# A hybrid decoder layer on one core: the corner of a triangular inverse started later between the products, its turned operand loaded first

## The chip, the cores and the metric

The kernel runs on one NeuronCore of a Trainium2 chip. The core has a matrix engine (TensorE, PE in the profile, with PEld for its weight loads), a vector engine (VectorE, DVE), a scalar engine (ScalarE, ACT), GpSimd (POOL) and a sync engine (SyncE, SP) that mostly issues DMA transfers. Each engine runs its own instructions in order, and semaphores order them between engines. The metric is the device time of one execution in microseconds (us). The kernel before took 2265.33 us, the median of three runs (2264.02, 2265.33 and 2266.41).

## The reference

The layer has 1024 tokens of width 1024. It is a SwiGLU half-step, then a mixer of three branches (an RWKV-7 recurrence, sliding-window attention, attention into 256 memory tokens) that are merged by sigmoid gates, then another SwiGLU half-step, with normalisation around each.

```python
g_a, g_b, g_c = _split(jax.nn.sigmoid(gate_logits + gate_b[l]), (D, D, D))
merged = (g_a * (y_a @ w_branch[l, 0]) + g_b * (y_b @ w_branch[l, 1])
          + g_c * (y_c @ w_branch[l, 2]))
```

The recurrence that gives `y_a` is, for each token,

```python
sa = jnp.einsum('bhvk,bhk->bhv', state, a_t)
state = (state * w_t[:, :, None, :] + sa[..., None] * b_t[:, :, None, :]
         + v_t[..., None] * k_t[:, :, None, :])
```

The kernel computes it in 16 chunks of 64 tokens. Within a chunk the terms in `sa` make a triangular system of 64 equations for each of 8 heads, so 128 inverses of 64 by 64 triangular matrices are needed before the chunks can be walked in turn.

## The kernel before, in words

All of this lies in `mixer`. After the projections that feed the recurrence come seven **pairs** of column strips (`win_pair`, numbers 0 to 6; the pairs from 3 on are gates, 24 and up in `WIN_PAIRS`). A pair is computed by a Strassen-like scheme: seven **products** ("b11", "b21", "t2", "t1", "t3", "b22", "t4"), each of 12 matmuls of 128 by 512 (four blocks of the contraction, three matmuls each in `mm3`, lines 376 to 378, which emulate full float32 by high and low parts). They accumulate in the PSUM tiles `px`, `py` and `pz`. When a product is done, `kept` (line 1425, ACT) copies a partial sum to a `part` tile, or `made` (line 1432, DVE, then 1435, ACT) adds it to a kept one and writes half of an output tile `att`. The output tiles are two per pair from a pool of two, so an `att` tile of one pair cannot be written before the store of the same tile of the pair before has landed (line 1454, SP). The weights of each product come through `operands`: a load of `w_raw` (line 290, SP, five buffers), for the Strassen sums three or four DVE additions (lines 326, 327, 328 and 332), a cast to `w_hi` (line 299, ACT) and a subtraction to `w_lo` (line 301, DVE), eight operands ahead of their use. A `w_raw` load is issued when the buffer is free, which is when the last `w_lo` made from it is done.

The inverses are built beside these products. `rwkv_invert` solves, on DVE, the two diagonal 32 by 32 blocks of all 128 matrices during pairs 0 to 3, stores them in `inv_d`, and stores one of them transposed in `turn_d`. `rwkv_corner` then makes the remaining corner block as a product of three 32 by 32 blocks on PE. It loads `up` (from `ab_d`), `low` (from `inv_d`) and `turned` (from `turn_d`), four transfers each on SP (line 1176), every one in runs of 32 numbers, 128 bytes. The matmuls are cut into eight **lumps**: four of `iturned` with `iup`, whose result ACT copies to `ihalf`, and four of `ilow` with `ihalf`, whose result `icorner` goes back into `inv_d` in four transfers on the ACT queue (line 1190). `win_pair` calls `between()` after each product, which gives one lump, and `issue_after` keeps the next product of the pair behind that lump. `CORNER = (4, 5)` puts the lumps into pair 4: one after each of its seven products, the eighth right behind the seventh.

Then the pool `chunks` is opened, pair 5 runs, `chunk_fetch` asks for the first two chunks' tiles (`f`, 640 KB, line 1195; `dinv`, the inverse, two transfers of 64 KB, line 1197), and pair 6 runs. `rwkv_chain` walks the 16 chunks: each step is a row of small matmuls (line 1210) and a transposition (line 1249) with short DVE, ACT and POOL work between, and while that runs, matmuls of two plain gate strips (`pgate`) fill PE.

What stands in which order on an engine is decided by a scheduler in the language's tile layer: program order by default, `high_priority` moves things ahead, `issue_after` and `keep_in_program_order` bind them, and a product that is ready may be pulled ahead of one that is not. The order of the built program is fixed; at run time each engine works down its list.

Of the kernel before, what the change touches and what calls it, by code (L numbers as in the profile page):

```python
# [1 line left out]

# [1 line left out]

# [41 lines left out]
BRANCHES = (0, 2, 1)  # L46
ATT_BLOCKS = (18, 19, 14, 15, 16, 17, 20, 21, 22, 23)
GATES_PLAIN = 2
CORNER = (4, 5)
GATES_FIRST = 10  # L50
GATES_EARLY = 12
LUMPS = (29, 52)
# [2 lines left out]
WIN_PAIRS = ((16, 17), (20, 21), (22, 23)) + tuple((24 + g, 25 + g) for g in range(GATES_PLAIN, GATES_FIRST, 2))  # L55
# [6 lines left out]
H = C // 2  # L62
# [168 lines left out]
class Builder:  # L231
# [934 lines left out]
    def rwkv_corner(self, pool, ab_d, inv_d, turn_d):  # L1166

        nc = self.nc
        flat = lambda d: d.rearrange("c p q s t -> (c p q) s t")
        groups = [slice(g * H, (g + 1) * H) for g in range(P // H)]  # L1170
        up, turned, low, half, corner = (pool.tile([P, H, H], F32, name="i" + n, bufs=1) for n in ("up", "turned", "low", "half", "corner"))
        urgent = lambda: self.tc.high_priority(offset=self.urgent)
        with urgent():
            for t, d in ((up, flat(ab_d)[:, :H, H:]), (low, flat(inv_d)[:, H:, H:]), (turned, turn_d)):
                for g in groups:
                    nc.sync.dma_start(t[g], d[g].rearrange("i s t -> s i t"))
        for w, x, out in ((up, turned, half), (half, low, corner)):
            for a in range(0, H, H // 4):
                if a % (H // 2) == 0:
                    ps = self.psum("corner").rearrange("p (i t) -> p i t", t=H)  # L1180
                with urgent():
                    for i in range(a, a + H // 4):
                        for g in groups:
                            mm = self.tc.keep_in_program_order(nc.tensor.matmul(ps[g, i % (H // 2)], w[g, i], x[g, i], start=True, stop=True))
                    if a % (H // 2):
                        nc.scalar.copy(out[:, a - H // 4 : a + H // 4], ps)
                yield mm
        with urgent():
            for g in groups:
                nc.scalar.dma_start(flat(inv_d)[g, :H, H:].rearrange("i s t -> s i t"), corner[g])  # L1190
# [549 lines left out]
    def mixer(self, u, cp, close_raws, att_d, gate_d, km_d, vm_d):  # L1740
        nc, tc, io = self.nc, self.tc, self.io
        pk_d = tc.dram_tile([NC_, P, NPAIR, 5 * C], F32, name="pk_d")
        ab_d = tc.dram_tile([NC_, NPAIR, 2, C, C], F32, name="ab_d")
        inv_d = tc.dram_tile([NC_, NPAIR, 2, C, C], F32, name="inv_d")
        turn_d = tc.dram_tile([P, H, H], F32, name="turn_d")
# [17 lines left out]
        with tc.tile_pool(reuse_waits="tile", name="gates", bufs=2) as gp:  # L1763
            out = lambda: gp.tile([P, T], F32, tag="gate", name="att", bufs=2)
            with sums, tc.tile_pool(reuse_waits="tile", name="mix_xa", bufs=4) as pools["xa"]:
                fs = self.mix_forms(u, forms, loads)
            with tc.tile_pool(reuse_waits="tile", name="inv", bufs=1) as pool:
# [9 lines left out]
                for _ in inverse:  # L1777
                    pass
            for i in range(1, CORNER[0]):
                self.win_pair(i, fs, out, att_d, gate_d)  # L1780
            with tc.tile_pool(reuse_waits="tile", name="corner", bufs=1) as pool:
                corner = self.rwkv_corner(pool, ab_d, inv_d, turn_d)
                for i in range(*CORNER):
                    self.win_pair(i, fs, out, att_d, gate_d, lambda: next(corner))
                for _ in corner:
                    pass
            chunks = contextlib.ExitStack()
            early = chunks.enter_context(tc.tile_pool(reuse_waits="tile", name="chunks", bufs=2))
            self.win_pair(CORNER[1], fs, out, att_d, gate_d)
            fetched = [self.chunk_fetch(early, c, pk_d, inv_d) for c in (0, 1)]  # L1790
            for i in range(CORNER[1] + 1, len(WIN_PAIRS)):
                self.win_pair(i, fs, out, att_d, gate_d)
            over.close()
            with chunks, tc.tile_pool(reuse_waits="tile", name="chain", bufs=2) as pool:
                y = pool.tile([P, NPAIR, T], F32, name="y", bufs=1)
# [274 lines left out]
```

## Time and profile before

| | |
|---|---|
| median of three runs | 2265.33 us (2264.02 to 2266.41) |
| the profiled execution | 2265.33 us, of which the span is 2263.3 us |
| busy in the span | PE 98%, PEld 81%, DVE 73%, ACT 46%, POOL 3% |
| chain that ended last | PE 91%, DVE 4%, DMA 2%, ACT 1% |
| DMA | 431.90 MB, 191 GB/s over the span |
| mean granted clock of TensorE | 0.996 |

The page of a profile gives busy times, the span cut into slices, the chain of work that ended last and the costliest groups of instructions. The other views are of the same execution: the waits (who waited for whom, in all, how often, the longest), the timeline (start, duration, engine, line, operation, output and inputs, and in brackets the idle time before and what ended it), and the windows (busy time of each engine in a stretch, with the granted clock as a share of full speed and the busy share of the DMA engines). A matmul's row shows its duration with its latency, so the pace of a product is read from the distance of its starts.

### The profile page before, as it was taken

Reading aid. Unit: us, or ns where it says so; the run is one execution under the profiler, and the core shown is the slowest. Engines: PE = TensorE matmul, PEld = TensorE weight load, DVE = VectorE, ACT = ScalarE, POOL = GpSimd, SP = SyncE. Lnnn points to the kernel's source line nnn. Section 1 sums busy time; section 2 is a strip of 40 time slices with the busy share of each in tenths; the row PEclk is TensorE's granted clock in tenths of the full one; section 3 lists DMA queues with packets and bytes.
Section 4 is the critical chain, followed back from the end, with each engine's and each line's share of the span. In section 5 each row is a group of like instructions: output and inputs, shape, how many; then the busy total and the mean of one; then the engine's idle time right before and its main releaser. Section 6 shows DMA issues by size and latency. Waiting matters only on the chain.

```text
span 2263.3 us, 34508 instructions
## 1 busy us (share of the span) xinstructions
PE 2228.9 (98%) x12304; PEld 1832.7 (81%) x12304; DVE 1642.9 (73%) x2761; ACT 1031.4 (46%) x1933; POOL 59.3 (3%) x114
## 2 busy tenths in 40 slices
PE   8999999999999999979999999999999999999998
PEld 6888888888887788868888887788888888888887
DVE  6988767766698888853667567784898886656576
ACT  6523333454556654334445454434663223345451
POOL 0000000000000000000331000000000000000000
PEclk9999999999999999989999999999999999999999
DMA  8565666686665356455437877564565552357663
GB/s 292 172 202 167 202 212 215 228 291 205 193 208 195 111 159 195 149 154 166 147 107 248 271 255 263 178 211 135 171 214 176 196 189 103 115 167 250 203 195 122
DMA packets 279132, 431.90 MB, mean 191 GB/s; under 512 B 58512, under 2 KB 96912, under 8 KB 278704
## 3 DMA queue, kind: packets, MB, share of 16 engines
q1 hardware_dynamic: 266160, 409.96, 56.0%
q10 hardware_dynamic: 12800, 19.73, 2.7%
q8 instruction: 97, 1.59, 0.3%
q14 instruction: 75, 0.61, 0.1%
HBM read 292.75 MB, written 135.79 MB: 189 GB/s over the span
## 4 chain that ended last, share of the span: by engine, by line
PE 91%; DVE 4%; DMA 2%; ACT 1%; issue 1%; SPq 1%; DVEq 0%; ACTq 0%
PE px L376 9%; PE px L378 9%; PE px L377 9%; PE po L376 6%; PE po L377 6%; PE po L378 6%; PE pz L376 4%; PE pz L377 4%; PE pz L378 4%; PE pgate L376 2%; PE pgate L378 2%; PE pgate L377 2%; PE pr L376 2%; PE pr L377 2%; PE pr L378 2%; PE pb L376 2%
## 5 line engine op out<-in xcount | busy, mean ns | idle before, releaser
L299 ACT CAST w_hi<-w_raw 128x512 fp32r<-128x512 f32 x608 | 377.0, 622 | 734.9 <-PE px L377 178.8
L301 DVE TENSOR_TENSOR w_lo<-w_raw,w_hi 128x512 fp32r<-128x512 f32 x608 | 418.6, 690 | 184.1 <-ACT w_hi L299 165.1
L376 PE MATMUL po<-u,w_hi 128*128 128x512 f32 (+1 forms) x476 | 180.9, 380 | 0.0
L378 PE MATMUL po<-u,w_lo 128*128 128x512 f32 (+1 forms) x476 | 180.9, 380 | 0.0
L377 PE MATMUL po<-u,w_hi 128*128 128x512 f32 (+1 forms) x476 | 180.9, 380 | 0.0
L376 PE MATMUL px<-u,w_hi 128*128 128x512 f32 x380 | 148.0, 390 | 0.8 <-DVE km L1595 0.8
L376 PE MATMUL pz<-u,w_hi 128*128 128x512 f32 x380 | 148.0, 389 | 0.0
L378 PE MATMUL px<-u,w_lo 128*128 128x512 f32 x380 | 147.9, 389 | 0.0
L377 PE MATMUL px<-u,w_hi 128*128 128x512 f32 x380 | 147.8, 389 | 0.0
L378 PE MATMUL pz<-u,w_lo 128*128 128x512 f32 x380 | 147.8, 389 | 0.0
L377 PE MATMUL pz<-u,w_hi 128*128 128x512 f32 x380 | 147.8, 389 | 0.0
L376 PE MATMUL px<-f,w_hi 128*128 128x512 f32 x352 | 137.1, 390 | 0.0
L378 PE MATMUL px<-f,w_lo 128*128 128x512 f32 x352 | 137.0, 389 | 0.0
L377 PE MATMUL px<-f,w_hi 128*128 128x512 f32 x352 | 136.9, 389 | 0.0
L485 DVE TENSOR_TENSOR u<-hid,u 128x512 fp32r<-128x512 f32 x114 | 78.5, 691 | 43.4 <-ACT u L484 42.2
L378 PEld LDWEIGHTS po<-u,w_lo 128*128 128x128 f32 x476 | 89.5, 188 | 17.1
L377 PEld LDWEIGHTS po<-u,w_hi 128*128 128x128 f32 x476 | 89.5, 188 | 17.0
L376 PEld LDWEIGHTS po<-u,w_hi 128*128 128x128 f32 x476 | 89.5, 188 | 16.8
L376 PE MATMUL pgate<-u,w_hi 128*128 128x512 f32 x256 | 103.0, 402 | 0.0
L378 PE MATMUL pgate<-u,w_lo 128*128 128x512 f32 x256 | 101.7, 397 | 0.0
L484 ACT CAST u<-hid 128x512 fp32r<-128x512 f32 x114 | 70.9, 622 | 65.1 <-DMA hid<-form_d 58.4
L377 PE MATMUL pgate<-u,w_hi 128*128 128x512 f32 x256 | 99.9, 390 | 0.0
(453 smaller groups left out, 5169.3 us busy)
## 6 DMA issues: line engine op xcount, KB each, us to landing
w_raw<-in_ffn_in SPq DMA_DIRECT2D x224, 256.0 KB
hid<-form_d SPq DMA_DIRECT2D x154, 256.0 KB
w_raw<-in_win SPq DMA_DIRECT2D x112, 256.0 KB
form_d<-g SPq DMA_DIRECT2D x88, 256.0 KB
w_raw<-ffn_sum_d SPq DMA_DIRECT2D x88, 256.0 KB
form_d<-h SPq DMA_DIRECT2D x66, 256.0 KB
w_raw<-in_ffn_out SPq DMA_DIRECT2D x66, 256.0 KB
first_d<-first SPq DMA_DIRECT2D x48, 256.0 KB
```

The lines of the kernel that those rows point to most:

```text
L299: self.nc.scalar.copy(hi, x)
L301: self.split_last = self.nc.vector.tensor_tensor(lo, x, hi.bitcast(F32), ALU.subtract)
L376: mm(out, wh, xh, start=first, stop=False, **kw)
L377: mm(out, wh, xl, start=False, stop=False, **kw)
L378: self.last_mm = mm(out, wl, xh, start=False, stop=last, **kw)
L484: self.nc.scalar.copy(hi, x)
L485: self.nc.vector.tensor_tensor(lo, x, hi.bitcast(F32), ALU.subtract)
```

## The change

`CORNER` becomes `(4, 4)`: its first number is still the pair at which the corner begins, its second is now a number of products. The lumps become a chain of four empty entries and then the corner's steps. Pairs 4 and 5 both draw from it after each product, so that the corner starts in the middle of pair 4 and runs on into pair 5. The pool of the corner's tiles stays open until pair 5 has been written down, the pool `chunks` is opened after it, and the first two chunks are fetched in the program just ahead of pair 6, the last. Inside `rwkv_corner` the loads are written `up`, `turned`, `low` where they were `up`, `low`, `turned`. The arithmetic is the same.

```diff
+import itertools
-CORNER = (4, 5)
+CORNER = (4, 4)
...
-            for t, d in ((up, flat(ab_d)[:, :H, H:]), (low, flat(inv_d)[:, H:, H:]), (turned, turn_d)):
+            for t, d in ((up, flat(ab_d)[:, :H, H:]), (turned, turn_d), (low, flat(inv_d)[:, H:, H:])):
                 for g in groups:
                     nc.sync.dma_start(t[g], d[g].rearrange("i s t -> s i t"))
...
             with tc.tile_pool(reuse_waits="tile", name="corner", bufs=1) as pool:
-                corner = self.rwkv_corner(pool, ab_d, inv_d, turn_d)
-                for i in range(*CORNER):
-                    self.win_pair(i, fs, out, att_d, gate_d, lambda: next(corner))
-                for _ in corner:
-                    pass
+                lumps = itertools.chain(itertools.repeat(None, CORNER[1]), self.rwkv_corner(pool, ab_d, inv_d, turn_d))
+                for i in range(CORNER[0], len(WIN_PAIRS) - 1):
+                    self.win_pair(i, fs, out, att_d, gate_d, lambda: next(lumps, None))
+                assert next(lumps, None) is None
             chunks = contextlib.ExitStack()
             early = chunks.enter_context(tc.tile_pool(reuse_waits="tile", name="chunks", bufs=2))
-            self.win_pair(CORNER[1], fs, out, att_d, gate_d)
             fetched = [self.chunk_fetch(early, c, pk_d, inv_d) for c in (0, 1)]
-            for i in range(CORNER[1] + 1, len(WIN_PAIRS)):
-                self.win_pair(i, fs, out, att_d, gate_d)
+            self.win_pair(len(WIN_PAIRS) - 1, fs, out, att_d, gate_d)
```

The scheduler makes more of this than the diff tells. Line numbers in the changed program are one higher up to the end of `rwkv_finish` and its neighbours (L376 is now L377).

**The corner's start, on PE.** Rows of matmuls with buffer numbers; only the first of each product's 12 is shown. `px_9254`, `py_9255`, `pz_9256` are pair 4's sums. Before:

```order
L376 MATMUL px_9254<-u_5952,w_hi_9119 128x512
...
L1184 MATMUL corner_9300<-iturned_9284,iup_9283 32x32 x32
L376 MATMUL py_9255<-u_5976,w_hi_9137 128x512
...
L1184 MATMUL corner_9300<-iturned_9284,iup_9283 32x32 x32
L376 MATMUL px_9254<-mix_form_8232,w_hi_9159 128x512
```

Now, with `px_9515` the first product of pair 5:

```order
L377 MATMUL px_9254<-mix_form_8248,w_hi_9195 128x512
...
L377 MATMUL px_9515<-u_5952,w_hi_9267 128x512
...
L1185 MATMUL corner_9376<-iturned_9360,iup_9359 32x32 x32
L377 MATMUL pz_9256<-u_6661,w_hi_9214 128x512
...
L1185 MATMUL corner_9376<-iturned_9360,iup_9359 32x32 x32
L377 MATMUL px_9254<-mix_form_8256,w_hi_9232 128x512
```

The first lump stood behind the first product of pair 4. It now stands behind five products of pair 4 and the first of pair 5, which was pulled ahead. Behind the first lump come "b22" of pair 4, the second lump, and "t4" of pair 4.

**The same place on SP**, where the rows are the issued transfers. Before, from the corner's loads to the first chunk tile:

```order
L1176 DMA iup<-ab_d 32x32x32 x4
L1176 DMA ilow<-inv_d 32x32x32 x4
L1176 DMA iturned<-turn_d 32x32x32 x4
L1454 DMA gate_d<-att 128x1024
L290 DMA w_raw<-in_win 128x512 x4
L1454 DMA gate_d<-att 128x1024 x2
L1195 DMA f<-pk_d 128x1280
```

Now:

```order
L1177 DMA iup<-ab_d 32x32x32 x4
L1177 DMA iturned<-turn_d 32x32x32 x4
L1177 DMA ilow<-inv_d 32x32x32 x4
L291 DMA w_raw<-in_win 128x512 x4
L1455 DMA gate_d<-att 128x1024 x3
L291 DMA w_raw<-in_win 128x512 x3
L1455 DMA gate_d<-att 128x1024
L291 DMA w_raw<-in_win 128x512 x5
L1455 DMA gate_d<-att 128x1024
L291 DMA w_raw<-in_win 128x512
L1196 DMA f<-pk_d 128x1280
```

The store of pair 3's second output tile stood right behind the corner's loads; four weight loads are ahead of it now. The first chunk tile stood behind four weight loads, and stands behind thirteen.

**The outputs of pair 4, on DVE.** `att<-py`, `att<-px` and `att<-pz` are line 1432 (now 1433) after the products "b21", "t3" and "b22". Before:

```order
L1432 TENSOR_TENSOR att<-py,part 128x512
L301 TENSOR_TENSOR w_lo<-w_raw,w_hi 128x512
L301 TENSOR_TENSOR w_lo<-part,w_hi 128x512
L301 TENSOR_TENSOR w_lo<-w_raw,w_hi 128x512
L1432 TENSOR_TENSOR att<-px,part 128x512
L301 TENSOR_TENSOR w_lo<-w_raw,w_hi 128x512
L1432 TENSOR_TENSOR att<-pz,part 128x512
```

Now:

```order
L302 TENSOR_TENSOR w_lo<-part,w_hi 128x512
L302 TENSOR_TENSOR w_lo<-w_raw,w_hi 128x512 x3
L1433 TENSOR_TENSOR att<-pz,part 128x512
L302 TENSOR_TENSOR w_lo<-w_raw,w_hi 128x512
L327 TENSOR_TENSOR part<-w_raw 128x512
L328 TENSOR_TENSOR w_raw<-w_raw 128x512
L329 TENSOR_TENSOR w_raw<-part,w_raw 128x512
L1433 TENSOR_TENSOR att<-px,part 128x512
```

`att<-px`, which reads what "t3" has summed and has to be done before "t4" may add to `px`, stood ahead of `att<-pz`; it stands behind it and behind four more instructions.

**The chain's last step on PE.** Before:

```order
L1249 MATMUL bkt<-ident,f 128x128 x4
L378 MATMUL pgate<-u,w_lo 128x512
L376 MATMUL pgate<-u,w_hi 128x512
L377 MATMUL pgate<-u,w_hi 128x512
L378 MATMUL pgate<-u,w_lo 128x512
L376 MATMUL pgate<-u,w_hi 128x512
L377 MATMUL pgate<-u,w_hi 128x512
L1210 MATMUL z<-sv,gz 64x64 x8
L1210 MATMUL y<-gz,uv 64x64 x8
```

Now:

```order
L1211 MATMUL z<-uv,bk 64x64 x8
L1250 MATMUL bkt<-ident,f 128x128 x4
L1211 MATMUL z<-sv,gz 64x64 x8
L1211 MATMUL y<-gz,uv 64x64 x8
L1211 MATMUL y<-f,sv 64x64 x8
```

Eleven `pgate` matmuls are pulled ahead into pair 6 (three behind its third product in the built order, eight behind its fourth). They are missing at the chain's end: the last step has none of its six, the step before has two, and one is missing behind the last step.

## The prediction

> **What bounds the kernel now.** I read the page first, then the waits of PE, then the windows and the timeline around the largest wait, and last the queues that the change reorders.
>
> ```profile
> PE 2228.9 (98%) x12304; PEld 1832.7 (81%) x12304; DVE 1642.9 (73%) x2761; ACT 1031.4 (46%) x1933; POOL 59.3 (3%) x114
> PE 91%; DVE 4%; DMA 2%; ACT 1%; issue 1%; SPq 1%; DVEq 0%; ACTq 0%
> PE corner L1184 <- DMA iturned<-turn_d: 11.7, 4, 10.2
> PE var L1336 <- DVE ysq_lo L1326: 0.8, 1, 0.8
> 1000.00:1010.00 10.00, 2.34 (x65) 1.88 (x66) 0.00 (x0) 0.00 (x0) 0.00 (x0) 0.53 1.08 153
> 1010.00:1020.00 10.00, 10.00 (x157) 7.62 (x157) 1.98 (x3) 2.93 (x5) 0.00 (x0) 0.79 0.09 28
> 1020.00:1030.00 10.00, 10.00 (x226) 7.73 (x225) 2.69 (x5) 3.56 (x6) 0.00 (x0) 1.00 0.16 54
> ```
>
> PE is busy for 98% of the span and carries 91% of the chain that ended last, so a stall of PE is paid in full. The largest is in the corner: 11.7 us, waiting for the gather of `turned`; the next one near it is 0.8 us. In the windows (PE, PEld, DVE, ACT and POOL busy, granted clock, DMA share) all engines stand still in 1000 to 1010 while DMA is full at 1.08, and the clock is 0.53 there and 0.79 in the next window: the stall also costs pace after it. The timeline gives both parts.
>
> ```profile
> 993.10 0.39 PE L376 MATMUL px<-u,w_hi 128*128 128x512 f32 x1
> 995.59 0.39 PE L378 MATMUL px<-u,w_lo 128*128 128x512 f32 x1
> 1006.19 0.31 PE L1184 MATMUL corner<-iturned,iup 32*32 32x32 f32 x2 [10.21 <-DMA iturned<-turn_d]
> 1008.58 1.05 PE L1184 MATMUL corner<-iturned,iup 32*32 32x32 f32 x58 [0.31 <-DMA iturned<-turn_d]
> 1009.57 0.80 PE L376 MATMUL py<-u,w_hi 128*128 128x512 f32 x1
> 1014.64 0.75 PE L1184 MATMUL corner<-iturned,iup 32*32 32x32 f32 x64
> 1018.28 0.75 PE L1184 MATMUL corner<-iturned,iup 32*32 32x32 f32 x64
> 1021.91 0.75 PE L1184 MATMUL corner<-iturned,iup 32*32 32x32 f32 x64
> ```
>
> A product is 12 matmuls; its first and last start 2.49 us apart, so one takes 2.49 / 11 = 0.2265 us and the product 2.72. From lump 3 to lump 4 a lump and a product take 1021.91 - 1018.28 = 3.63, so a lump costs 0.91. The first product of pair 4 is through at 993.10 + 2.72 = 995.82. From there to lump 3 stand two lumps and two products, 7.26 us of work; they took 1018.28 - 995.82 = 22.46. **The stall costs 15.2 us**, 2.35 of them because the product between lumps 1 and 2 took 1014.64 - 1009.57 = 5.07 instead of 2.72.
>
> **The change, part by part.** *The later start.* The first lump now stands behind six products (five of pair 4 and the first of pair 5, which the scheduler pulls ahead): 993.10 + 6 x 2.72 = 1009.42. Even as the last of the twelve gathers, `turned` had landed by 1008.6 (the last bracket above).
>
> ```profile
> 992.79 5.19 SPq L1176 DMA_DIRECT2D iup<-ab_d  x4
> 998.02 3.41 SPq L1176 DMA_DIRECT2D ilow<-inv_d  x4
> 1001.47 3.76 SPq L1176 DMA_DIRECT2D iturned<-turn_d  x4
> 1005.34 0.86 SPq L1454 DMA_DIRECT2D gate_d<-att  x1
> 1016.12 14.82 SPq L290 DMA_DIRECT2D w_raw<-in_win  x4
> ```
>
> *The order of loads* puts `turned` 3.45 us earlier (1001.47 - 998.02), so by about 1005.2, with 4 us to spare. `low` takes its place, by 1008.6, and is needed with lump 5, some 10 us later. The full 15.2 us go, in the clock too: eight lumps of work stay, and the two that now stand back to back were back to back before.
>
> *What takes its place, at "t4" of pair 4.* DVE must have read `px` (`att<-px`) before "t4" may add to it, and in the new order that row stands behind `att<-pz`, a `w_lo` and three weight sums. All of these wait for "b22". The pace of DVE is in these rows:
>
> ```profile
> 993.73 0.69 DVE L301 TENSOR_TENSOR w_lo<-w_raw,w_hi 128x512 fp32r<-128x512 f32 x1 [1.86 <-ACT w_hi L299]
> 994.33 0.69 DVE L326 TENSOR_TENSOR part<-w_raw 128x512 f32<-128x512 f32 x1
> 997.05 0.69 DVE L327 TENSOR_TENSOR w_raw<-w_raw 128x512 f32<-128x512 f32 x1
> 997.77 0.69 DVE L328 TENSOR_TENSOR w_raw<-part,w_raw 128x512 f32<-128x512 f32 x1
> 1025.55 0.75 PE L1184 MATMUL corner<-ilow,ihalf 32*32 32x32 f32 x64
> 1025.71 0.69 DVE L1432 TENSOR_TENSOR att<-px,part 128x512 f32<-128x512 f32 x1 [2.57 <-PE px L378]
> 1026.32 0.68 DVE L301 TENSOR_TENSOR w_lo<-w_raw,w_hi 128x512 fp32r<-128x512 f32 x1
> ```
>
> Independent instructions start 0.60 apart, dependent ones 0.72, and the first behind a product starts about 0.25 after the product's last slot (lump 5 at 1025.55 follows that slot, which ends at 1025.46). "b22" now runs from 1009.42 + 0.91 = 1010.33 to 1013.05. So `att<-pz` starts at 1013.30, `w_lo` at 1013.90, the sums at 1014.50, 1015.10 and 1015.82, `att<-px` at 1016.42, done with its 0.69 at 1017.11. PE, past lump 2, wants "t4" at 1013.05 + 0.91 = 1013.96. **New stall: 3.2 us.** Before, `att<-px` had a lump and "b22" as its cover, 3.63 us. Behind the waiting DVE instruction only later weights queue, none of which PE needs within those 3 us.
>
> The output tile that `att<-px` writes must also have been stored by pair 3, and that store has moved behind four weight loads. The fourth goes out when the `w_lo` of pair 5's last operand is done, which follows the sixth product: 1009.42 + 1.31 (a `w_lo` starts at 1026.32 in the rows above and is done at 1027.00, against its product's last slot at 1025.46, with 0.23 off since no `att` stands ahead of it) = 1010.7, so the store goes at about 1011.1. How long a store of this size takes:
>
> ```profile
> 1059.69 0.43 SPq L1454 DMA_DIRECT2D gate_d<-att  x1
> 1063.83 0.69 DVE L1432 TENSOR_TENSOR att<-py,part 128x512 f32<-128x512 f32 x1 [1.09 <-DMA gate_d<-att]
> ```
>
> 4.1 us, so it lands at 1015.2, 1.2 us before DVE gets there. DVE's order decides, the store is the next limit behind it: an `att<-px` put back ahead of `att<-pz` would still wait till 1015.2, for a stall of 1.9. The bounds of this term are 0 (if DVE's wait is covered in a way I don't see) and 5.6, which is 3.2 and the 2.35 of lost pace again.
>
> The clock bears on that upper bound: the 10.2 us gap brought it to 0.53, the 0.8 us gap is not followed by a slow stretch, and nothing lies between. The Trainium skill ("TensorE: Matmul & The Clock Gate", section "What's actually happening") says that the array falls to half rate after an idle window of about 3.4 us, on windows that run free. By that rule a 3.2 us stall just stays at full rate, and one that is a little longer pays up to 2.35 more.
>
> *The fill of the chain.* Eleven `pgate` matmuls run in pair 6, where PE has no gap, and are missing behind the chain's last steps. What they cover there:
>
> ```profile
> 1093.36 0.86 DVE L1301 TENSOR_TENSOR sv<-ts,sw 64x256 f32<-64x256 f32 x2
> 1094.13 0.40 PE L377 MATMUL pgate<-u,w_hi 128*128 128x512 f32 x1
> 1094.46 0.69 PE L1210 MATMUL z<-sv,gz 128*64 128x64 f32 x16
> ```
>
> `z<-sv` may start when `sv` is done at 1094.22 and starts at 1094.46, so a step without fill ends only 0.2 earlier. Pulled ahead: 11 x 0.2265 = 2.5 us. Won back: 0.2 in each of two steps and one slot of 0.23 behind the last, 0.6. **Cost 1.9 us**; bounds 0 and 2.5.
>
> *The chunk tiles.* The first one was asked for 38 us before its use and is now behind thirteen weight loads.
>
> ```profile
> 1034.36 1.32 SPq L1195 DMA_DIRECT2D f<-pk_d  x1
> 1065.48 0.33 SPq L290 DMA_DIRECT2D w_raw<-in_win  x1
> 1072.34 0.68 PE L1210 MATMUL y<-center,f 64*64 64x64 f32 x16
> 1077.13 0.51 PE L1210 MATMUL y<-center,f 64*64 64x64 f32 x11
> ```
>
> The thirteenth load follows pair 6's fourth product by 1.35; between that product and the chain stand eight `pgate` and three products, 8 x 0.2265 + 3 x 2.72 = 9.97 us. So `f` goes out 8.3 us before the chain. 640 KB against the store's 512 KB in 4.1 us is an estimated 5.1, slack 3. The second `f` follows a load that waits for pair 6's fifth product and goes 3 us before the chain; it is needed 4.8 after the chain's start (1077.13), slack 2.7. Both cost nothing; if that cover is gone, each us late is a us of stall.
>
> **Sum**: -15.2 + 3.2 + 1.9 = -10.1. The profiled execution took 2265.33, the median itself (its span is 2263.3): 2265.33 - 10.1 = **2255.2**.
>
> **Rivals.** *No new stall*: "t4" finds `px` read. For it: every other product of this stretch does. Against: the fixed order on DVE. -15.2 + 1.9: 2252.0. *The new stall takes pace*: 2.35 more, 2257.6. For it: the clock rows; against: the gap is a third of that one. *The change doesn't do what it says*: the gathers land after 1009.4 still, since DMA is full until 1010 and four weight loads now follow directly. It takes 4 us of delay to `turned` before anything is lost; at 7 us, 3 us of stall are back: 2258.2. *Slower than before*: the chain waits for its chunk tiles. Price: the lateness of the first `f`. It breaks even at 3 + 10.1 = 13 us later than worked out, an `f` of 18 us; it is slower by 5 us at 23 us, 2270. For it: the twelve gathers took from 992.79 to 1008.6. Against: those are 128-byte runs, the chunk tiles are not, and the windows of pair 6's time are not full:
>
> ```profile
> 1060.00:1080.00 20.00, 20.00 (x181) 16.26 (x180) 9.79 (x20) 10.19 (x21) 4.31 (x8) 1.00 0.72 241
> ```
>
> **How the numbers follow.** Forecast 60%, no new stall 17%, stall with lost pace 10%, gathers late 8%, chunk tiles late 5%. The tell-apart bound of 0.2% is 4.5 us, so faster means below 2260.8. The first three cases are faster, 87%; of the late gathers about half (a stall back of less than 5.6 us), and of the late tiles a part, are too: 91% together. Same 6%, slower 3%. The range reaches from nearly all of the 15.2 us won (2250.5) to the stall with lost pace and some lateness of a gather or tile (2259.5).
>
> **What would show it.** Right: the waits of PE no longer name `iturned`; they name `att` (line 1433) with about 3.2 us before "t4" of pair 4; the clock stays at 1.00 between 1000 and 1030; the chain starts at 1072.34 - 15.2 + 3.2 + 2.5 = 1062.8; in its last two steps PE waits for `sv` for about 2 us together. Wrong: a wait of PE for `f`, `dinv` or `ilow`, a slow clock behind the new stall, or a time above 2259.5.

## The result and the profile after

The changed kernel takes 2256.48 us, the median of six runs (2255.78 to 2257.27); the kernel before, run beside it on the same chip, takes 2264.98 (2262.71 to 2266.41, six runs). The ratio is 0.9964, with a 95% interval of 0.9951 to 0.9976: 8.5 us faster, where 10.1 were forecast. The profiled execution is the slowest of the six, 2257.27 us. The page's head and busy times, and the list of what PE waited for (in all, how often, the longest):

```profile
span 2255.6 us, 34511 instructions
PE 2227.7 (99%) x12304; PEld 1832.2 (81%) x12304; DVE 1642.0 (73%) x2761; ACT 1028.9 (46%) x1933; POOL 58.8 (3%) x114
PE px L377 <- DVE att L1433: 3.4, 1, 3.4
PE z L1211 <- DVE sv L1302: 1.8, 2, 1.1
```

PE has the same number of instructions and is busy for about the same time; the span is 7.7 us shorter. The wait for `iturned` (11.7 us before) is gone from the list, and two new ones have come: 3.4 us for `att`, and 1.8 us for `sv` in the chain. The windows of the corner (PE, PEld, DVE, ACT and POOL busy, granted clock, DMA share) and the timeline of PE there:

```profile
1000.00:1010.00 10.00, 10.00 (x106) 8.11 (x105) 2.68 (x5) 3.95 (x7) 0.00 (x0) 1.00 1.08 176
1010.00:1020.00 10.00, 6.64 (x84) 5.12 (x83) 4.08 (x7) 2.53 (x4) 0.00 (x0) 0.84 0.39 138
1020.00:1030.00 10.00, 10.00 (x286) 7.77 (x286) 3.15 (x5) 4.26 (x8) 0.00 (x0) 0.99 0.23 82
...
1008.94 0.75 PE L1185 MATMUL corner<-iturned,iup 32*32 32x32 f32 x64
1012.57 0.75 PE L1185 MATMUL corner<-iturned,iup 32*32 32x32 f32 x64
1016.68 0.65 PE L377 MATMUL px<-mix_form,w_hi 128*128 128x512 f32 x1 [3.36 <-DVE att L1433]
1021.20 1.29 PE L1185 MATMUL corner<-iturned,iup 32*32 32x32 f32 x128
```

The window in which PE was busy for only 2.34 us before, 1000 to 1010, is now full at clock 1.00. What is left of the loss comes later and is smaller: PE stands for 3.36 us ahead of "t4" of pair 4, and then the clock is below full. From its first start to the next lump "t4" takes 1021.20 - 1016.68 = 4.52 us. The product between the first two lumps takes 2.95 from its first start to the next lump (1012.57 - 1008.94 = 3.63 from lump to lump, less the lump's own 0.68 to the product's first start). So 1.57 us of pace are lost behind the gap.

DVE's timeline shows what the gap is made of:

```profile
1012.68 0.69 DVE L1433 TENSOR_TENSOR att<-pz,part 128x512 f32<-128x512 f32 x1 [2.47 <-PE pz L379]
1013.29 0.68 DVE L302 TENSOR_TENSOR w_lo<-w_raw,w_hi 128x512 fp32r<-128x512 f32 x1
1013.88 0.69 DVE L327 TENSOR_TENSOR part<-w_raw 128x512 f32<-128x512 f32 x1
1014.61 0.69 DVE L328 TENSOR_TENSOR w_raw<-w_raw 128x512 f32<-128x512 f32 x1
1015.33 0.69 DVE L329 TENSOR_TENSOR w_raw<-part,w_raw 128x512 f32<-128x512 f32 x1
1015.94 0.68 DVE L1433 TENSOR_TENSOR att<-px,part 128x512 f32<-128x512 f32 x1
```

This is the row of six that the prediction laid out, without a pause; the last one has no bracket, so it waited for nothing but its turn.

The last third of the change, pair 6 and the chain: the `pgate` matmuls alone in pair 5's end and pair 6 (first window, its busy times those of PE, PEld and ACT), then all engines over the chain, after and, in the last row, before.

```profile
1030.00:1064.10 34.10, 2.82 (x11) 2.07 (x11) 0.00 (x0) 1.00 0.51 150
1064.10:1187.10 123.00, 119.83 (x1998) 99.03 (x1998) 76.62 (x175) 57.18 (x128) 45.52 (x69) 1.00 0.44 136
...
1072.30:1195.50 123.20, 122.17 (x2009) 100.97 (x2009) 76.71 (x175) 57.54 (x128) 45.94 (x69) 1.00 0.42 126
```

Eleven `pgate` matmuls have gone into pair 6 and are missing in the chain (1998 against 2009), and PE stands there for 3.2 us instead of 1.0. The chain starts at 1064.20, the first row below. The first reader of the first chunk tile, on POOL, starts 3.0 us ahead of it (second row). Its bracket names `dinv`, but what it reads is `f`, so `f` was there by then. The second tile's first reader starts 0.9 us ahead of PE's first use (third and fourth row). No wait of PE names `f`, `dinv` or `ilow`.

```profile
1064.20 0.68 PE L1211 MATMUL y<-center,f 64*64 64x64 f32 x16
1061.21 0.85 POOL L1222 COPY gz<-f 64x256 f32<-64x256 f32 x2 [202.43 <-DMA dinv<-inv_d]
1067.94 0.83 POOL L1222 COPY gz<-f 64x256 f32<-64x256 f32 x2 [3.77 <-DMA f<-pk_d]
1068.83 0.27 PE L1211 MATMUL y<-center,f 64*64 64x64 f32 x2
```

### The profile page after: what moved, and what is told of

It reads as the page before. It is cut to its first block, busy times and chain, and to the rows that moved or that the text cites. A ratio compares the mean times of both kernels' runs of the same rounds, so it can differ in the third digit from the quotient of the medians.

```text
span 2255.6 us, 34511 instructions
## 1 busy us (share of the span) xinstructions
PE 2227.7 (99%) x12304; PEld 1832.2 (81%) x12304; DVE 1642.0 (73%) x2761; ACT 1028.9 (46%) x1933; POOL 58.8 (3%) x114
## 4 chain that ended last, share of the span: by engine, by line
PE 51%; DMA 1%; DVE 1%; ACT 1%; issue 0%; SPq 0%; DVEq 0%; ACTq 0%
PE px L377 4%; PE px L379 4%; PE px L378 4%; PE po L377 3%; PE po L378 3%; PE po L379 3%; PE pgate L377 2%; PE pgate L378 2%; PE pgate L379 2%; PE pz L377 2%; PE pz L379 2%; PE pz L378 2%; PE pb L377 2%; PE pb L378 2%; PE pb L379 2%; PE pw L378 1%
## 5 line engine op out<-in xcount | busy, mean ns | idle before, releaser
L377 PE MATMUL po<-u,w_hi 128*128 128x512 f32 (+1 forms) x476 | 180.9, 380 | 0.0
L377 PE MATMUL px<-u,w_hi 128*128 128x512 f32 x380 | 147.9, 389 | 0.8 <-DVE km L1596 0.8
L377 PE MATMUL pz<-u,w_hi 128*128 128x512 f32 x380 | 148.1, 390 | 0.0
L377 PE MATMUL px<-f,w_hi 128*128 128x512 f32 x352 | 137.1, 390 | 0.0
L377 PE MATMUL pgate<-u,w_hi 128*128 128x512 f32 x256 | 103.3, 403 | 0.0
L377 PEld LDWEIGHTS po<-u,w_hi 128*128 128x128 f32 x476 | 89.5, 188 | 16.8
```

The source lines that it names most:

```text
L377: mm(out, wh, xh, start=first, stop=False, **kw)
```

## The experiments

Times in this section are compared through the kernel before that ran beside each group: 2263.99 us for the first four, 2263.75 for the last four.

**One part alone: the order of the loads.** The kernel before, with

```diff
-            for t, d in ((up, flat(ab_d)[:, :H, H:]), (low, flat(inv_d)[:, H:, H:]), (turned, turn_d)):
+            for t, d in ((up, flat(ab_d)[:, :H, H:]), (turned, turn_d), (low, flat(inv_d)[:, H:, H:])):
```

> The kernel before with one part of the change alone: `turned` loaded ahead of `low`, the first lump still behind one product of pair 4. Theory (the later start carries the gain): PE reaches the first lump near 996 and `turned` lands some 3.45 us earlier than the 1006.2 to 1008.6 of before, so PE still waits about 8 us for iturned, the clock still falls, and the time is 3 to 4 us below the kernel before (ratio about 0.9985). Rival (the order of the loads carries it): the wait for iturned is gone or under 3 us, and the time is 8 us or more below. No stall at att, since the DVE order of pair 4 is nearly the one of before.

2261.85 us, 2.1 below the kernel before, ratio 0.9988 (0.9979 to 0.9996). What PE waited for, and two lumps of its timeline:

```profile
PE corner L1184 <- DMA iturned<-turn_d: 7.6, 4, 5.8
1002.09 0.28 PE L1184 MATMUL corner<-iturned,iup 32*32 32x32 f32 x2 [5.77 <-DMA iturned<-turn_d]
1014.86 0.75 PE L1184 MATMUL corner<-iturned,iup 32*32 32x32 f32 x64
```

The wait is 7.6 us where 8 were expected. The first product of pair 4 starts at 993.43 in this execution and lump 3 at 1014.86, 21.43 us apart; before it was 1018.28 - 993.10 = 25.18. That is 3.75 won, near the 3.45 by which the load moved. By these rows the order alone is worth a quarter of the stall. The medians show 2.1 us, under the 3 to 4 that were expected, with an interval of 0.9 to 4.8 us that holds both.

**The other part alone: the later start.** The changed kernel, with the old order of loads:

```diff
-            for t, d in ((up, flat(ab_d)[:, :H, H:]), (turned, turn_d), (low, flat(inv_d)[:, H:, H:])):
+            for t, d in ((up, flat(ab_d)[:, :H, H:]), (low, flat(inv_d)[:, H:, H:]), (turned, turn_d)):
```

> The changed kernel with the old order of loads: `turned` is the last of the twelve gathers again. Theory: it lands by about 1008.1 to 1008.6 and PE reaches the first lump at 1008.9, so there is no wait for iturned above 0.5 us. In this kernel's DVE order two weight sums that need no product stand ahead of the read of `pz`, and the read of `px` comes right behind it and one w_lo, so the new stall at `t4` of pair 4 should be 1.5 to 2.5 us instead of 3.4: the time is that of the changed kernel or up to 2.5 us below it (2254 to 2257). Rival (the order of loads is needed as well): a wait for iturned of 2 us or more, and a time 2 us or more above the changed kernel.

2255.62 us, 8.4 below the kernel before, ratio 0.9959 (0.9947 to 0.9971): as fast as the whole change. PE has no wait for `iturned`. The rows of PE, DVE and SP around "t4":

```profile
1017.24 0.50 PE L377 MATMUL px<-mix_form,w_hi 128*128 128x512 f32 x1 [2.22 <-DVE att L1433]
1020.20 1.29 PE L1185 MATMUL corner<-iturned,iup 32*32 32x32 f32 x128
...
1014.37 0.69 DVE L1433 TENSOR_TENSOR att<-pz,part 128x512 f32<-128x512 f32 x1 [1.02 <-PE pz L379]
1014.98 0.68 DVE L302 TENSOR_TENSOR w_lo<-w_raw,w_hi 128x512 fp32r<-128x512 f32 x1
1016.49 0.69 DVE L1433 TENSOR_TENSOR att<-px,part 128x512 f32<-128x512 f32 x1 [0.83 <-DMA gate_d<-att]
...
1012.30 9.33 SPq L1455 DMA_DIRECT2D gate_d<-att  x3
```

The new stall is here too, 2.22 us. In this order DVE's read of `px` has only one `w_lo` ahead of it, and now the bracket names the store: issued at 1012.30, it holds DVE until 1016.49, 4.2 us. So behind DVE's order stands the store of pair 3's tile, as the prediction had said. "t4" takes 2.96 us to the next lump: a gap of 2.22 cost no pace. From the first product of pair 4 to the chain this kernel takes 1063.20 - 994.22 = 68.98 us, 2.7 less than the whole change (71.67). The medians don't show that: the interval of this ratio is 2.7 us wide to each side, and this profile loses time elsewhere (it is the slowest of the five executions).

**What causes the new stall: one store moved.** In `win_pair` of the changed kernel, with an offset of 400 the store goes out behind the gathers, with 1000 ahead of them:

```diff
         for f, t in zip(strips, (first, second)):
-            nc.sync.dma_start(gate_d[f - 24] if f >= 24 else att_d[ATT_ROW[f]], t)
+            with self.tc.high_priority(offset=400) if i == CORNER[0] - 1 and t is second else contextlib.nullcontext():
+                nc.sync.dma_start(gate_d[f - 24] if f >= 24 else att_d[ATT_ROW[f]], t)
```

> The changed kernel with one store moved: the store of pair 3's second tile goes out right behind the twelve gathers and ahead of the four weight loads. PE's order stays; on DVE `att<-px` of pair 4 now stands ahead of the three weight sums instead of behind them. Theory (the new stall is DVE's order, set by when that store is planned): `att<-px` is done near 1014.5, 2.1 us earlier, so the stall falls from 3.4 to about 1.3 us, and the product behind it keeps its 2.7 us instead of 4.5 since a gap that short costs no clock: 3 to 4 us below the changed kernel (about 2253). Rival (the store is not the cause): the stall stays above 3 us. Rival for the clock: any gap there costs pace, `t4` still takes over 4 us, and only 2 us are won.

> The changed kernel with the same store moved ahead of the twelve gathers. On DVE `att<-px` of pair 4 now stands ahead of `att<-pz` and two w_lo, as in the kernel before. Theory: PE does not wait for att at `t4` at all, its clock stays at 1.00, and the time is that of the changed kernel less 3.4 us of stall and 1.8 us of lost pace: about 2251.3. The gathers go out 1 to 2.4 us later, since the store has to wait for its tile; `turned` then lands near 1007, before PE's 1008.9. Rival (the later gathers take it back): a wait for iturned or ilow of over 1 us, and a time above 2253.

Behind the gathers: 2252.26 us, ratio 0.9945 (0.9933 to 0.9957). Ahead of them: 2250.57 us, ratio 0.9939 (0.9927 to 0.9951), the fastest kernel of the study, 13.4 us below the kernel before. The first two rows are of PE with the store behind the gathers, the last three of PE with it ahead:

```profile
1015.37 0.50 PE L377 MATMUL px<-mix_form,w_hi 128*128 128x512 f32 x1 [1.30 <-DVE att L1433]
1018.34 1.29 PE L1185 MATMUL corner<-iturned,iup 32*32 32x32 f32 x128
...
1009.03 0.75 PE L1185 MATMUL corner<-iturned,iup 32*32 32x32 f32 x64
1012.67 0.75 PE L1185 MATMUL corner<-iturned,iup 32*32 32x32 f32 x64
1016.30 1.29 PE L1185 MATMUL corner<-iturned,iup 32*32 32x32 f32 x128
```

The stall falls from 3.36 to 1.30 and then to nothing: lump to lump is 3.63 us with the store ahead. "t4" takes 2.97 us behind the 1.30 us gap. With the store ahead of them the gathers start 2 us later than in the changed kernel (994.25 against 992.25), and PE still waits for none. The rivals (the store is not the cause; the later gathers take it back) are out, and 13.4 us is what the prediction had worked out for the case without a new stall, 15.2 - 1.9 = 13.3.

**The fill of the chain.** In the changed kernel the products of the two gates wait for the chain's first matmuls:

```diff
-                mm(at(ps, p, 1 - q, W4), n["f"][ROWS[q], p, 4, :], self.center[ROWS[q]])
+                self.centred = mm(at(ps, p, 1 - q, W4), n["f"][ROWS[q], p, 4, :], self.center[ROWS[q]])
...
         values(n, self.psum("y"))
+        self.started = self.centred
...
-        self.project(self.strip("win", 24 + g), u, ps)
+        w = self.strip("win", 24 + g)
+        with self.tc.issue_after(self.started.ins) if g >= GATES_FIRST else contextlib.nullcontext():
+            self.project(w, u, ps)
```

> The changed kernel with the products of gates 10 and 11 held behind the first matmuls of the chain, so that none of the eleven pgate matmuls runs in pair 6; everything up to pair 6 stays, the stall at `t4` too. Theory: the two waits of PE for `sv` at the chain's last steps (1.8 us together) are filled again, and pair 6 is 2.5 us shorter: the time falls by 1.9 to 2.2 us against the changed kernel, to about 2254.4. Rival (the missing fill costs nothing, because the chain's own steps set its end): the waits for sv go, but the time stays within 0.5 us of the changed kernel.

2256.25 us, ratio 0.9963 (0.9951 to 0.9975): no gain over the changed kernel's 0.9964. The largest entry of what PE waited for between 1030 and 1190 us, and the windows of `pgate` alone and of the chain:

```profile
PE px L377 <- ACT part L1427: 1.6, 1, 1.6
1030.00:1063.50 33.50, 0.00 (x0) 0.00 (x0) 0.00 (x0) 1.00 0.52 150
1063.50:1187.10 123.60, 122.31 (x2009) 100.97 (x2009) 76.77 (x175) 57.52 (x128) 47.46 (x74) 1.00 0.45 136
```

The edit did what it should: no `pgate` in pair 6, 2009 matmuls in the chain again, no wait for `sv`. But pair 6 now has a wait of 1.6 us, for ACT's copy of `px` to `part`. In the changed kernel eight of the eleven matmuls stood at this place, 8 x 0.2265 = 1.8 us, and covered that. From the first product of pair 4 to the chain 0.64 us are won (1063.61 - 992.58 = 71.03 against 1064.20 - 992.53 = 71.67), and the chain itself, from its first matmul to the last of `var` behind it, is 0.55 longer (122.72 against 122.17). The theory falls, and the rival, which expected no gain because the chain sets its own end, was right on the time and only half on the reason.

**Both mended**, the store ahead of the gathers and the gates' products held:

> The changed kernel with both mended: the store of pair 3's second tile ahead of the gathers, and the gates' products held behind the chain's first matmuls. Theory (the two losses are independent, and nothing else stands between the stall removed and the gain): no wait for att, none for sv, and 1.9 to 2.2 us less than the 2250.57 of the store alone, about 2248.5. Against the kernel before that is 15 to 16 us, the whole of the corner's stall. Rival (they share a limit): less than 1 us below the store alone.

2251.73 us, ratio 0.9942 (0.9930 to 0.9954), not below the store alone. Again PE has no wait for `att` or `sv` and one for `part`, of 1.0 us. The rival's number came out, but since holding the gates gained nothing by itself either, this run can't tell whether the two losses are independent. It shows that the second edit mends nothing.

**The price of a gap in clock.** The kernel with the store behind the gathers, with the read of `px` done three and six times:

```diff
-                    V.tensor_tensor(t, ps, x, ALU.add)
+                    for _ in range(3 if i == CORNER[0] and (n, h) == (1, 1) else 1):
+                        V.tensor_tensor(t, ps, x, ALU.add)
```

> The kernel with the store right behind the gathers (stall at `t4` 1.3 us, no clock lost), and DVE's read of `px` done three times over instead of once, so that PE waits about 1.3 + 2 x 0.72 = 2.7 us there; the sum is the same. Theory (the clock is set in stretches of 3.4 us, and a stretch in which PE stands nearly all of the time halves the next one): 2.7 us is too short for most positions of such a stretch, the clock stays at 1.00, `t4` takes 2.7 to 3.0 us and the time is 1.4 us above the kernel with the single read. Rival (every gap costs pace in proportion): `t4` takes about 4.1 us.

> The same with the read of `px` done six times over; three weight sums come in between by DVE's order, so PE waits 1.3 + 5 x 0.72 and one or two sums of 0.6, about 5.5 us. Theory (stretches of 3.4 us): one stretch is idle for at least 2.7 us, so at least one half-rate stretch follows, that is 1.7 us lost on top of the 5.5, and at most two, 3.4 us: the time is 5.9 to 7.6 us above the kernel with the single read. Rival (loss in proportion to the gap, 1.55 us at 3.4): 2.5 us lost and no fixed length of the slow stretch.

Three reads: 2255.35 us, 3.3 above the single read, ratio to the kernel before 0.9960 (0.9946 to 0.9975). Six: 2259.12, 7.1 above, ratio 0.9979 (0.9969 to 0.9990). "t4" with three reads, some of the 1 us windows around it, and then the same with six:

```profile
1016.70 0.50 PE L377 MATMUL px<-mix_form,w_hi 128*128 128x512 f32 x1 [2.75 <-DVE att L1434]
1021.22 1.29 PE L1185 MATMUL corner<-iturned,iup 32*32 32x32 f32 x128
1017.00:1018.00 1.00, 1.00 (x5) 0.81 (x4) 0.94 (x2) 0.45 (x1) 0.00 (x0) 0.91 0.00 0
1018.00:1019.00 1.00, 1.00 (x4) 0.72 (x4) 0.69 (x1) 0.00 (x0) 0.00 (x0) 0.50 0.00 0
1021.00:1022.00 1.00, 1.00 (x93) 0.78 (x94) 0.45 (x1) 1.00 (x2) 0.00 (x0) 0.88 0.00 0
...
1019.47 0.79 PE L377 MATMUL px<-mix_form,w_hi 128*128 128x512 f32 x1 [5.88 <-DVE att L1434]
1024.39 1.29 PE L1185 MATMUL corner<-iturned,iup 32*32 32x32 f32 x128
1016.00:1017.00 1.00, 0.00 (x0) 0.00 (x0) 0.97 (x3) 0.00 (x0) 0.00 (x0) 0.97 0.50 205
1023.00:1024.00 1.00, 1.00 (x4) 0.82 (x3) 0.00 (x0) 0.00 (x0) 0.00 (x0) 0.62 0.00 0
```

My expectation for the shorter gap was wrong: 2.75 us halved the clock, and "t4" took 4.52 us, as after 3.36. A loss in proportion, the rival, fits no better: 4.1 was its number, and 2.22 us had cost nothing. What holds is the fixed length. A window mean of 0.91 is full rate for 0.82 us and half for 0.18, so the half rate begins at 1017.82 with three reads and, by the mean of 0.88, ends at 1021.24: 3.42 us. With six reads it runs from 1016.94 to 1023.76, two such stretches. By the rows the longer gap and the pace cost 2.75 - 1.30 + 1.57 = 3.0 us with three reads and 5.88 - 1.30 + (4.92 - 2.95) = 6.6 with six, near the 3.3 and 7.1 measured, so the expectation for six (5.9 to 7.6) holds.

## Why the prediction came out

**The corner's stall, -15.2: right.** The wait for `iturned` is gone. The kernel without any new stall measures 13.4 against 13.3, so this term and the fill's 1.9 hold together. That they meet to 0.1 us is in part chance: from the first product of pair 4 to the chain that kernel takes 1059.65 - 992.62 = 67.03 us where the kernel before took 79.24, 12.2 less, and the two terms of this stretch give 15.2 - 2.5 = 12.7. The later start alone gives all of the gain, the order alone 2.1 us, and the 4 us that the order was to give `turned` to spare were not needed.

**The new stall, 3.2: right in place, cause and size.** 3.36 us, at "t4" of pair 4, behind the six rows of DVE that were named. Moving the one store takes it away, and the delay-only kernel shows the second limit that the prediction had put behind it, the store's landing.

**Its price in clock: the term that was mis-sized.** The forecast took the clock to stay at 1.00 and put "the new stall takes pace" at 2.35 us and a chance of 10%. The pace was lost, and it is 1.57, so one of the prediction's own signs of being wrong, "a slow clock behind the new stall", came up; the result lies between that rival's 2257.6 and the forecast's 2255.2. What was said against it, that the gap is a third of the old one, decides nothing, since the loss comes in whole stretches of 3.42 us and not in proportion to the gap. There was also a gap between those of 0.8 and 10.2 us, where the prediction had seen none: in the kernel before, PE stands for 1.26 us ahead of 780.70, and the clock is 1.00 behind it. The Trainium skill ("TensorE: Matmul & The Clock Gate", section "What's actually happening") has a window of 4096 cycles, 3413 ns, that runs free, and half rate after at least one idle window. The length agrees with 3.42 us here. The idle window, read as an empty one, does not: the prediction concluded from it that 3.2 us would stay at full rate, and 2.75 us did not.

**The fill, 1.9: right in size, half wrong in reason.** From the first product of pair 4 to the chain the kernel takes 71.67 us where it took 1072.34 - 993.10 = 79.24, 7.57 less. The prediction's own terms for this stretch are -15.2 + 3.2 + 2.5 = -9.5; the 1.57 of pace and 0.16 of stall make most of the 1.93 between. So the 2.5 us of eleven `pgate` matmuls are paid there. But the step "pair 6, where PE has no gap" failed. It had none before, where pair 6's first products stood among those of pair 5; in the changed order it has one of 1.6 us, and the `pgate` matmuls only fill it. The loss is therefore not to be had back by holding them. Of the 0.6 us won back at the chain's end, 0.25 came (122.42 us before, 122.17 after); with the store moved 0.5 to 0.6 came (121.88 behind the gathers, 121.85 ahead of them).

**The chunk tiles, 0: right.** The first has at least the 3.0 us that were worked out, the second 0.9 instead of 2.7, and PE waits for neither. The rival "slower than before" didn't come up.

**The sum.** -15.2 + 3.36 + 1.57 + 2.5 - 0.25 = -8.0, against 8.5 in the medians and 7.7 between the two profiled spans. The profiled executions also differ by 0.6 us ahead of pair 4 (993.10 against 992.53, in favour of the changed kernel) and by 0.7 behind `var` (against it), where the program has the same work; in the other profiles that last part varies by more than this, and what does it is open.

## What to carry to other kernels

When a step is moved out of a stall, ask what it had covered for its neighbours: here a lump had given DVE time to read a PSUM tile, and two pairs had covered each other's copies. Where a DVE read comes late although its input is ready, look for the store that must first free its output tile; one store put ahead of a block of loads was worth more (4.9 us beyond the whole change) than the order of the loads alone (2.1). A gap of PE does not cost in proportion to its length: as soon as it halves the clock for one stretch of 3.4 us it costs up to half of that, 1.7 us, besides (1.57 here).

## What the runs showed of the hardware

The slow stretches of the clock begin on a grid of 3.413 us that runs through the whole execution. In the changed kernel's profile the clock first falls within 1016 to 1017 and again within 2245 to 2246:

```profile
1016.00:1017.00 1.00, 0.32 (x1) 0.32 (x2) 0.62 (x2) 0.29 (x1) 0.00 (x0) 0.93 0.25 98
2245.00:2246.00 1.00, 0.43 (x4) 0.35 (x4) 0.16 (x1) 0.47 (x2) 0.00 (x0) 0.83 0.77 235
```

In the kernel before, the half rate lasts from 1000.50 to 1014.16 (the 1 us windows from 1000 and from 1014 have means of 0.75 and 0.92): four stretches of 3.41 us. In the changed kernel the two falls are, by the means, at 1016.86 and 2245.66, 1228.80 us apart, which is 360 stretches of 3.4133. With three reads they are at 1017.82 and 2246.62, again 1228.80 apart. Laid over the gaps, the grid fits which of them cost pace: with three reads the stretch before the slow one had 2.3 of its 3.41 us idle; the 1.30 us gap lay within one stretch and cost nothing; the 2.22 us gap of the delay-only kernel was cut by the grid into 1.25 and 0.97 and cost nothing. So the point from which a stretch counts as idle lies, among dense matmuls, between 1.3 and 2.3 us of 3.41. By this reading it depends on where a gap of 2 to 3 us falls whether it costs pace; no run here moved a gap of one length along the grid, so that is argued and not shown.

Three cases are outside this, all in stretches with matmuls other than 128x512. In the delay-only kernel the clock also fell at 1391.74, for one stretch, behind a gap of only 0.84 us among the attention's matmuls of 64 rows:

```profile
1390.43 2.01 PE L101 MATMUL sc<-kd,qs 64*128 64x256 f32 x8 [0.84 <-DVE pt L169]
1392.00:1393.00 1.00, 1.00 (x4) 0.54 (x3) 0.42 (x2) 1.00 (x6) 0.00 (x0) 0.50 1.07 291
```

The same gap is in the profiles before and after, at full clock. The second is the fall at 2245.66 above: in the stretch before it, 2242.25 to 2245.66, PE stands for only 1.1 us, but behind the last 128x256 matmul it runs just eight of 128x1. The third is in the kernel before: the stretch from 1007.33 to 1010.75, at half rate and filled mostly with a lump of 32x32 matmuls, has 0.9 us idle and is still followed by half rate. That such matmuls count for less than dense ones would fit, but it was not tried.
